# Three float32r score passes, half of a 31-tap convolution on GpSimd, and an earlier second GLU in a two-block layer kernel

## The chip, the cores and the metric

The kernel runs on one core of a Trainium2 chip. The metric is the device time of one execution in microseconds, the median of several runs. Everything is float32 at the interface; products are done in float32r, in pairs of a high and a low part, or in plain fp32.

## The reference, cut to what matters

Two transformer layers run over 512 tokens of width 1024. The change lies in the second layer's mixer. Its input projection gives a gated 3-tap convolution branch, a GLU branch with a 31-tap causal depthwise convolution over 256 channels, and eight heads of stick-breaking attention of width 64:

```
a_b, a_c, a_h, b_glu, q, k, v = split(rmsnorm(x) @ w_in)
y_a = a_b * causal_dwconv(a_c * a_h, w_conv_a)                  # 3 taps, 256 channels
g   = b_glu[:, :256] * sigmoid(b_glu[:, 256:])
g   = causal_dwconv(g, w_conv_b) + b_conv_b                     # 31 taps, 256 channels
y_b = silu(layernorm(g, ln_b_g, ln_b_b))
for each head and each block of 128 queries:
    z = q k^T / 8;  mask = key < query
    log_1m = where(mask, log_sigmoid(z) - z, 0)
    a = where(mask, exp(log_sigmoid(z) + sum of log_1m over later keys), 0)
    y_c = a @ v
x = x + concat(y_a, y_b, y_c) @ w_out;  x = x + relu(rmsnorm(x) @ w_ff1)^2 @ w_ff2
```

## The kernel before, in words

Weights come in tiles of 512 KB on SyncE's DMA queue (four staging buffers `wst`). Each tile is split into two float32r parts: ScalarE casts the high part `whi` (L113), VectorE subtracts to get the low part `wlo` (L114). A product with a weight tile is three float32r passes for each K tile of 128: high by high, high by low, low by high. Eight K tiles make one accumulation in a PSUM bank.

Engines run their own queues in order. The framework puts the instructions of the program in each engine's queue and adds the waits; a tile with a tag and a number of buffers makes a later writer wait for the last reader of the buffer.

The stick-breaking stage is written as interleaved generators. `sb_scores(h)` makes one head's weights, one step for each of four query tiles j of 128 x 128(j+1) scores. TensorE makes the scores `z` from `QF` and `KF` in plain fp32 (L937; it runs as two instructions) and adds the mask by a bf16 product with the identity (L938). ScalarE takes Abs, Exp and Ln of them (L942 to L944), VectorE makes log sigmoid in `sbL` (L946) and sums along the keys with a scan into `sbe` (L947), GpSimd zeroes the last column of `sbP` (L949), and ScalarE takes the last Exp (L950). `sb_values(h)` transposes the weights on TensorE, splits them into `PTh` and `PTl` (ScalarE and VectorE) and multiplies by the values `VB`; the last key tile goes through plain fp32 copies, `PTf` and `VB3`, L964. `pv_evac` adds the halves of the result `o` into `sby`.

Between these steps the generator `fill` puts independent work on TensorE, one K tile (three 512-column products) a step: the values of all heads (32 steps), then q and k of head pairs 1 to 3 (16 each), the second GLU (16), the two gated convolutions (24 each) and a part of the output projection (16): 160 in all. Thirty-two of them run beside head 0's scores, then 16 in each of the heads 0 to 7. The first pair's q and k and the first GLU are made before the stage.

The 31-tap convolution of one channel half `a` is a first tap (`tensor_scalar`, L1039) and 30 more (`scalar_tensor_tensor` of G, a tap's weight and `cb`, L1041), all on VectorE. `conv_taps` issues them one after another: three in each of the four steps before head 0, two in each of four steps of a head, half 1 behind half 0. At head 5 the rest is issued, and `ln_steps` transposes `cb` on TensorE (L1048) for the LayerNorm. `gate_steps` uses the buffers `gac` and `gam`.

```
fill = sequence(v_steps(), pair_steps(1), glu_steps(1), pair_steps(2), pair_steps(3), gate_steps(0),
                gate_steps(1), half_steps(yT, w_out_2, [4, 5, 0, 1], fin_add, 0))
for h in range(8):
    for j in range(4):
        steps(values); steps(fill, 2); conv_taps(1)
        steps(scores); steps(values); steps(fill, 2); conv_taps(1)
```

Of the kernel before, what the change touches and what calls it, by code (L numbers as in the profile page):

```python
# [20 lines left out]
def kernel(  # L21
# [42 lines left out]
    x = x[0]  # L64
# [35 lines left out]
    # the tensor engine's clock rises under load: products of zeros while the inputs are on their way  # L100
# [42 lines left out]
    def proj_T(acc, w, hT, cols=slice(0, 128), ts=slice(0, 512)):  # L143
        """acc[c, tok] = w[:, cols]^T h^T, the weights stationary."""
        wh, wl = w
        xh, xl = hT
        nk = wh.shape[1]
        for k in range(nk):
            mm(acc[:, ts], wh[:, k, cols], xh[:, k, ts], start=k == 0, stop=False)  # L149
            mm(acc[:, ts], wh[:, k, cols], xl[:, k, ts], start=False, stop=False)  # L150
            mm(acc[:, ts], wl[:, k, cols], xh[:, k, ts], start=False, stop=k == nk - 1)  # L151
# [5 lines left out]
    def k_steps(acc, w, hT):  # L157
        """the same, in steps of one K tile"""
# [6 lines left out]
    def first_tiles(tiles, ahead=()):  # L165
        """The first products after a norm: all of the first 256 tokens, while the others are still on their way."""
# [12 lines left out]
    def nat_mm(aT, acc, t, chunks, mid=lambda: None, cols=slice(None)):  # L179
        """acc[tok tile t, c] = sum_k a^T[k]^T w[k]; chunks: (list of k, split weights)"""  # L180
# [10 lines left out]
    def nat_steps(aT, acc, t, chunks):  # L191
        """nat_mm in steps of one K tile"""
# [17 lines left out]
    def natural(aT, w, ks, fin, c0=0, parts=None):  # L210
        """fin(t, half, acc) for both halves of 1024 columns, token tile by token tile."""
        for half in range(2):
            nat_half(aT, w, ks, fin, half, c0, parts)

    def nat_half(aT, w, ks, fin, half, c0=0, parts=None):
# [4 lines left out]
        for t in range(4):  # L220
            if t == 3 and half and parts:
                # in two, so that less is left to do after the last product
# [12 lines left out]
    def half_sq(src, half, st):  # L235
        """mean of squares of one half row; eps goes in with the first half"""
# [22 lines left out]
    def norm_T(t, g, hT):  # L259
        """RMS norm of token tile t of the residual, transposed into hT."""  # L260
# [18 lines left out]
    # transposes that wait for their norm: products that need not wait go first  # L279
# [9 lines left out]
    # =====================  block 1: mixers  =====================  # L289
# [86 lines left out]
    # transposed, with a row of ones for the bias  # L376
# [23 lines left out]
    def r_proj(hd):  # L400
        """x (1 + tanh(x / 2)) = 2 silu(x) of this head's output gate, natural layout"""
# [244 lines left out]
    def nsa_scores(h, bi):  # L646
        """softmax weights of one branch, gated; a step per query tile"""
# [27 lines left out]
    def nsa_values(h, bi):  # L675
        """the branch's weighted values, on top of the other branches'; a step per key tile and its products"""
# [46 lines left out]
    def merge_gates():  # L723
        """the gates of both mixers, in steps of one K tile"""
# [15 lines left out]
    # mn's tiles 2 p, 2 p + 1 take the place of the queries of heads 2 p, 2 p + 1  # L740
# [39 lines left out]
    for m in range(8):  # L780
# [3 lines left out]
        # the gated sum of both branches: one half of silu's and one of the gates' tanh form  # L784
# [7 lines left out]
    def post_norm_T(t, half, src, f, g, g_next, hT, st, eng):  # L792
        """x[t] += rms_norm(src) * g, then the next norm; src is one half of a token tile's row."""
# [22 lines left out]
    # =====================  block 1: FFN  =====================  # L816
    pc, tc3 = pool("pc")
    # 4 KB each: the first weights of block 2, then parts of its mixers' output
# [3 lines left out]
    # constants of block 2's mixers  # L822
# [66 lines left out]
    # =====================  block 2: mixers  =====================  # L889
    p3, t3 = pool("p3")  # L890
    # y^T as hi / lo: K tiles 0-1 the gated conv, 2-3 the GLU conv, 4-7 the attention
# [5 lines left out]
    QF, KF = {}, {}  # L897
    VB = [base.tile([128, 8, 2, 64], F32R, name="VB", tag="gain" if t < 2 else "xn", bufs=2) for t in range(4)]
    VB3 = t3("VB3", shape=(128, 8, 64))
# [4 lines left out]

    def pair_qk(i, accs):
        QF[i], KF[i] = t3("QF", bufs=2), t3("KF", bufs=2)
        A.activation(QF[i], accs[0], AF.Copy, scale=0.125)
        A.copy(KF[i], accs[1])

    def pair_steps(i):  # L910
        accs = []
        yield from tile_steps(accs, 1280 + i * 128)
        QF[i] = t3("QF", bufs=2)
        A.activation(QF[i], accs[0], AF.Copy, scale=0.125)
        yield from tile_steps(accs, 1792 + i * 128)
        KF[i] = t3("KF", bufs=2)
        A.copy(KF[i], accs[1])

    def v_steps():
        chunks = [([k, k + 1], load(w_in_2, k, 2, 2304, 512)) for k in range(0, 8, 2)]  # L920
        for t in range(4):
# [4 lines left out]
            if t == 3:  # L926
                A.copy(VB3, src)

    def sb_scores(h):
        """stick-breaking weights of one head, a step per query tile"""  # L930
# [3 lines left out]
        for j in range(4):  # L934
            n = 128 * (j + 1)
            z = ps("s", "z")
            mm(z[:, 0:n], QF[i][r, j * 128:(j + 1) * 128], KF[i][r, 0:n], start=True, stop=False)  # L937
# [7 lines left out]
            # log sigmoid(z); then -log a(s) = (z(s+1) - log a(s+1)) - log sigmoid(z(s)), from the masked end  # L945
# [3 lines left out]
            P.memset(p[:, n - 1:n], 0.0)  # L949
# [4 lines left out]
    def sb_values(h):  # L954
        """the head's output: a step per key tile and its products, those one tile behind"""
# [6 lines left out]
        def products(b, ph, pl):  # L962
            if b == 3:
                mm(o[0:64, 384:512], VB3[:, h, :], ph, start=False, stop=False)  # L964
                return
# [5 lines left out]
        for b in range(4):  # L971
# [4 lines left out]
            if b < 3:  # L976
                ph = t3("PTh", F32R, bufs=2)
                pl = t3("PTl0", F32R) if b == 0 else t3("PTl", F32R, bufs=2)
                split_psum(ph[:, 0:n], pl[:, 0:n], pt[:, 0:n])
                parts.append((b, ph, pl))  # L980
                pl0 = pl if b == 0 else pl0
            else:
                pf = t3("PTf", shape=(128, 128))
                A.copy(pf, pt[:, 0:n])
                parts.append((b, pf, None))
# [8 lines left out]
        pv_evac(o, sby[0][r], t3("pvt", shape=(64, 512)))  # L994
# [15 lines left out]
    def log_sigmoid(dst, src, e):  # L1010
        """min(x, 0) - ln(1 + exp(-|x|))"""
# [5 lines left out]
    def sigmoid(src):  # L1017
        th = t3("gth")
# [17 lines left out]
    def conv_b(a, k):  # L1036
        src = G[a][:, 2 + k:514 + k]
        if k == 0:
            V.tensor_scalar(cb[a], src, cwb[:, a, 0:1], cvec[:, 0, a:a + 1], op0=OP.mult, op1=OP.add)  # L1039
        else:  # L1040
            V.scalar_tensor_tensor(cb[a], src, cwb[:, a, k:k + 1], cb[a], OP.mult, OP.add)  # L1041

    def ln_steps():
        ln = []
        for t in range(4):
# [8 lines left out]
            # the convolution's inputs are used up  # L1054
# [15 lines left out]
    def gate_steps(a):  # L1070
# [5 lines left out]
        m = t3("gam", shape=(128, 544))  # L1076
# [13 lines left out]
    taps = [(a, k) for a in range(2) for k in range(31)]  # L1090

    def conv_taps(n):
        for _ in range(n):
            if taps and taps[0][0] in ready:
                conv_b(*taps.pop(0))
# [13 lines left out]
    fill = sequence(v_steps(), pair_steps(1), glu_steps(1), pair_steps(2), pair_steps(3), gate_steps(0),  # L1109
# [7 lines left out]
    for h in range(8):  # L1117
        scores = sb_scores(h + 1) if h < 7 else iter(())
        values = sb_values(h)
        for j in range(4):  # L1120
            steps(values)
            steps(fill, 2)
# [7 lines left out]
            steps(fill, 2)  # L1130
# [18 lines left out]
    # =====================  block 2: FFN  =====================  # L1149
# [87 lines left out]
```

## Time and profile before

| | |
|---|---|
| Median of three runs | 1508.88 us (1506.49, 1508.88, 1509.02) |
| Span of the profiled execution | 1504.9 us (its own time is not listed apart) |
| TensorE busy | 1487.9 us, 99% |
| VectorE busy | 765.6 us, 51% |
| ScalarE busy | 606.6 us, 40% |
| GpSimd busy | 62.9 us, 4% |
| The stick-breaking stage | about 937 to 1107 us |

The busy share is an average over stages with other limits: VectorE's 51% is far higher in the stage that the change touches. Matmuls are pipelined and their recorded ends are modelled, so the distance between starts tells more of TensorE than the durations. In the rows below the unit is the microsecond unless a mean is given in ns.

### The profile page before, as it was taken

The numbers are of one execution on the slowest core, as the hardware profiler recorded it, in microseconds if no ns is written. First come the engines' busy times: TensorE is split into PE (matmuls) and PEld (weight loads), VectorE is DVE, ScalarE is ACT, GpSimd is POOL, SyncE is SP. The second block draws the span as 40 slices with busy tenths as digits, with TensorE's granted clock in tenths as the row PEclk, the third lists the DMA queues.
The fourth block names the chain that finished last, engine by engine and source line by source line (L and its number), as shares of the span: only waits on it lengthen the run. The fifth ranks groups of instructions, "written<-read, shape, count | busy, mean of one in ns | idle before, by whom it ended". The sixth has DMA issues, their size and how long they took to land.

```text
span 1504.9 us, 18389 instructions
## 1 busy us (share of the span) xinstructions
PE 1487.9 (99%) x7220; PEld 1200.7 (80%) x7220; DVE 765.6 (51%) x1258; ACT 606.6 (40%) x1081; POOL 62.9 (4%) x177
## 2 busy tenths in 40 slices
PE   8999999999999999999999999999999999999998
PEld 6788888787788898878888888666689888888886
DVE  5244456867655463233333445979756344243343
ACT  6333224666632342322222334577734224142233
POOL 2000002000000010000000021000100000000000
PEclk9999999999999999999999999999999999999999
DMA  8242222221134243242243322211133242242321
GB/s 237 64 112 57 71 71 70 57 57 44 55 112 139 85 128 97 75 123 84 71 125 95 116 70 72 84 56 57 56 98 99 71 126 87 67 127 84 101 82 56
DMA packets 181278, 133.09 MB, mean 88 GB/s; under 512 B 11765, under 2 KB 157239, under 8 KB 181192
## 3 DMA queue, kind: packets, MB, share of 16 engines
q1 hardware_dynamic: 181192, 131.92, 30.2%
q8 instruction: 57, 0.93, 0.3%
q14 instruction: 29, 0.24, 0.1%
HBM read 129.80 MB, written 2.10 MB: 88 GB/s over the span
## 4 chain that ended last, share of the span: by engine, by line
PE 94%; DVE 2%; POOL 1%; ACT 1%; issue 1%; SPq 0%; DMA 0%; POOLq 0%; ACTq 0%; DVEq 0%
PE ps L149 13%; PE ps L151 13%; PE ps L150 13%; PE nat L187 9%; PE nat L186 9%; PE nat L185 9%; PE ps L162 4%; PE ps L161 4%; PE ps L160 4%; PE z L937 1%; PE pt L700 1%; PE ps L187 1%; PE ps L185 1%; PE ps L186 1%; PE o L693 1%; PE tp L273 1%
## 5 line engine op out<-in xcount | busy, mean ns | idle before, releaser
L113 ACT CAST whi<-wst 128x1024 fp32r<-128x1024 f32 (+1 forms) x229 | 239.1, 1046 | 493.6 <-PE ps L150 196.2
L114 DVE TENSOR_TENSOR wlo<-wst,whi 128x1024 fp32r<-128x1024 f32 (+1 forms) x229 | 279.5, 1222 | 287.1 <-ACT whi L113 283.4
L149 PE MATMUL ps<-hTh,whi 128*128 128x512 f32 (+1 forms) x880 | 331.4, 377 | 0.0
L150 PE MATMUL ps<-hTl,whi 128*128 128x512 f32 (+1 forms) x880 | 330.2, 375 | 0.0
L151 PE MATMUL ps<-hTh,wlo 128*128 128x512 f32 (+1 forms) x880 | 329.4, 374 | 0.0
L151 PEld LDWEIGHTS ps<-hTh,wlo 128*128 128x128 f32 x880 | 165.7, 188 | 31.9 <-DVE wlo L114 0.2
L149 PEld LDWEIGHTS ps<-hTh,whi 128*128 128x128 f32 x880 | 165.7, 188 | 31.6
L150 PEld LDWEIGHTS ps<-hTl,whi 128*128 128x128 f32 x880 | 165.8, 188 | 30.9
L187 PE MATMUL nat<-whi,al 128*128 128x512 f32 (+1 forms) x440 | 171.7, 390 | 0.0
L186 PE MATMUL nat<-wlo,ah 128*128 128x512 f32 (+1 forms) x440 | 171.4, 389 | 0.0
L185 PE MATMUL nat<-whi,ah 128*128 128x512 f32 (+1 forms) x440 | 170.9, 388 | 0.0
L160 PE MATMUL ps<-hTh,whi 128*128 128x512 f32 x240 | 98.0, 408 | 0.0
L186 PEld LDWEIGHTS nat<-wlo,ah 128*128 128x128 f32 x440 | 82.8, 188 | 18.6
L185 PEld LDWEIGHTS nat<-whi,ah 128*128 128x128 f32 x440 | 82.8, 188 | 18.3
L187 PEld LDWEIGHTS nat<-whi,al 128*128 128x128 f32 x440 | 82.8, 188 | 17.5
L161 PE MATMUL ps<-hTl,whi 128*128 128x512 f32 x240 | 96.2, 401 | 0.0
L162 PE MATMUL ps<-hTh,wlo 128*128 128x512 f32 x240 | 95.8, 399 | 0.0
L1087 DVE TENSOR_TENSOR xt<-xt,nat 128x512 f32<-128x512 f32 x43 | 29.5, 686 | 98.9 <-PE nat L187 97.6
L162 PEld LDWEIGHTS ps<-hTh,wlo 128*128 128x128 f32 x240 | 45.3, 189 | 8.8
L240 POOL TENSOR_SCALAR sq<-sq 128x1 f32<-128x1 f32 x28 | 9.4, 335 | 1015.9 <-ACT junk L238 1015.5
L865 DVE TENSOR_TENSOR sg<-sg,ps 128x512 f32<-128x512 f32 x22 | 15.2, 689 | 70.6 <-PE ps L151 69.9
L160 PEld LDWEIGHTS ps<-hTh,whi 128*128 128x128 f32 x240 | 45.4, 189 | 6.5
(351 smaller groups left out, 2194.8 us busy)
## 6 DMA issues: line engine op xcount, KB each, us to landing
wst<-in_w_in_dram SPq DMA_DIRECT2D x70, 512.0 KB, 3.9
wst<-in_w_ff_dram SPq DMA_DIRECT2D x64, 512.0 KB, 4.0
wst<-in_w_ffn_gate_dram SPq DMA_DIRECT2D x22, 512.0 KB, 4.0
wst<-in_w_ffn_up_dram SPq DMA_DIRECT2D x22, 512.0 KB, 4.0
wst<-in_w_ffn_down_dram SPq DMA_DIRECT2D x22, 512.0 KB, 3.8
wst<-in_w_out_dram SPq DMA_DIRECT2D x16, 512.0 KB, 3.9
xt<-in_x_dram SPq DMA_DIRECT2D x8, 512.0 KB, 3.6
wst<-in_w_proj_gla_dram SPq DMA_DIRECT2D x8, 512.0 KB, 3.6
```

The source lines that it names most:

```text
L113: A.copy(hi, st)
L114: lo_eng[0].tensor_tensor(out=lo, in0=st, in1=hi.bitcast(F32), op=OP.subtract)
L149: mm(acc[:, ts], wh[:, k, cols], xh[:, k, ts], start=k == 0, stop=False)
L150: mm(acc[:, ts], wh[:, k, cols], xl[:, k, ts], start=False, stop=False)
L151: mm(acc[:, ts], wl[:, k, cols], xh[:, k, ts], start=False, stop=k == nk - 1)
L160: mm(acc, w[0][:, k], hT[0][:, k], start=k == 0, stop=False)
L161: mm(acc, w[0][:, k], hT[1][:, k], start=False, stop=False)
L162: mm(acc, w[1][:, k], hT[0][:, k], start=False, stop=k == 7)
L185: mm(acc, ah[:, s], wh[:, j, cols], start=i == 0, stop=False)
L186: mm(acc, ah[:, s], wl[:, j, cols], start=False, stop=False)
L187: mm(acc, al[:, s], wh[:, j, cols], start=False, stop=i == len(seq) - 1)
L1087: V.tensor_tensor(X[t][:, HALF[half]], X[t][:, HALF[half]], acc, OP.add)
```

## The change

Queries and keys are split into high and low float32r parts (`QH`, `QL`, `KH`, `KL`), and a score tile is three float32r passes instead of one fp32 product. The last key tile of the values goes the same float32r way as the others; `VB3` and `PTf` go. The zeroed column of `sbP` is written by VectorE. Channel half 0 of the 31-tap convolution is done on GpSimd, each tap as a multiply into `tap` and an add into `cb`; half 1 stays on VectorE; `conv_taps` issues one tap of each half that is ready. The second GLU goes ahead of pair 1 in `fill`, and head 0 takes 32 steps of `fill`, the other heads 14 each. Some tiles share buffers (`pvt` with `PTl0`, `gam` with `gth`, `tap` with `gac`). The other lines of the diff only take comments out.

```
+    def split_q(i, acc):
+        QF[i] = t3("QH", F32R, bufs=2), t3("QL", F32R, bufs=2)
+        split_psum(*QF[i], acc, scale=0.125)
+    def split_k(i, acc):
+        KF[i] = t3("KH", F32R, bufs=2), t3("KL", F32R, bufs=2)
+        split_psum(*KF[i], acc)
...
-            if t == 3:
-                A.copy(VB3, src)
...
-            mm(z[:, 0:n], QF[i][r, j * 128:(j + 1) * 128], KF[i][r, 0:n], start=True, stop=False)
+            for a, b in ((0, 0), (0, 1), (1, 0)):
+                mm(z[:, 0:n], QF[i][a][r, j * 128:(j + 1) * 128], KF[i][b][r, 0:n], start=a + b == 0, stop=False)
...
-            P.memset(p[:, n - 1:n], 0.0)
+            V.memset(p[:, n - 1:n], 0.0)
...
-            if b == 3:
-                mm(o[0:64, 384:512], VB3[:, h, :], ph, start=False, stop=False)
-                return
...
-        pv_evac(o, sby[0][r], t3("pvt", shape=(64, 512)))
+        pv_evac(o, sby[0][r], t3("pvt", shape=(64, 512), tag="PTl0"))
...
+        eng = V if a else P
         if k == 0:
-            V.tensor_scalar(cb[a], src, cwb[:, a, 0:1], cvec[:, 0, a:a + 1], op0=OP.mult, op1=OP.add)
+            eng.tensor_scalar(cb[a], src, cwb[:, a, 0:1], cvec[:, 0, a:a + 1], op0=OP.mult, op1=OP.add)
+        elif a:
+            V.scalar_tensor_tensor(cb[a], src, cwb[:, a, k:k + 1], cb[a], OP.mult, OP.add)
         else:
-            V.scalar_tensor_tensor(cb[a], src, cwb[:, a, k:k + 1], cb[a], OP.mult, OP.add)
+            tap = t3("tap", tag="gac")
+            P.tensor_scalar(tap, src, cwb[:, a, k:k + 1], None, op0=OP.mult)
+            P.tensor_tensor(out=cb[a], in0=cb[a], in1=tap, op=OP.add)
...
-    fill = sequence(v_steps(), pair_steps(1), glu_steps(1), pair_steps(2), pair_steps(3), gate_steps(0),
+    fill = sequence(v_steps(), glu_steps(1), pair_steps(1), pair_steps(2), pair_steps(3), gate_steps(0),
...
-            steps(fill, 2)
+            steps(fill, 2 if h else 4)
...
-            steps(fill, 2)
+            steps(fill, 2 - j % 2 if h else 4)
```

TensorE's queue at the widest score tile of head 0 (`z` from keys and queries, `identb` and `smask` the mask, then the values' projection), the piece of the difference:

```order
-L937 MATMUL z<-KF,QF 128x512
-L938 LDWEIGHTS identb
-L938 MATMUL z<-smask,identb 128x128
+L940 MATMUL z<-KH,QH 128x512
+L940 MATMUL z<-KL,QH 128x512
+L940 MATMUL z<-KH,QL 128x512
+L941 LDWEIGHTS identb
+L941 MATMUL z<-smask,identb 128x128
```

The one fp32 product has become three passes at the same place; the mask stays behind them.

GpSimd's queue at the start of the stage (`sq` and `rstd` belong to the norm before it, `sbP` are weight tiles, `G_7399` is half 1's input), before:

```order
L949 MEMSET sbP_7987 128x1
L1031 MEMSET G_7399 128x32
L1077 MEMSET gam 128x32
L240 TENSOR_SCALAR sq<-sq 128x1
L245 TENSOR_TENSOR rstd<-sq 128x1
L246 TENSOR_TENSOR rstd<-rstd,nhalf 128x1
L949 MEMSET sbP_8041 128x1
```

and now (`G_7397` is half 0's input and `cb_7395` its sum, `G_7398` half 1's input):

```order
L1026 MEMSET G_7398 128x32
L240 TENSOR_SCALAR sq<-sq 128x1
L245 TENSOR_TENSOR rstd<-sq 128x1
L246 TENSOR_TENSOR rstd<-rstd,nhalf 128x1
L1035 TENSOR_SCALAR cb_7395<-G_7397,cwb,cvec 128x512
L1040 TENSOR_SCALAR tap<-G_7397,cwb 128x512
L1041 TENSOR_TENSOR cb_7395<-cb_7395,tap 128x512
L1040 TENSOR_SCALAR tap<-G_7397,cwb 128x512
L1041 TENSOR_TENSOR cb_7395<-cb_7395,tap 128x512
```

The one-column memsets have gone from this queue, and the pair of multiply and add follows the first tap thirty times in a row; the memset of `gam` stands behind them.

VectorE's queue in head 1, from the sum of head 0's values (`sby`) on, before:

```order
L644 TENSOR_TENSOR sby<-o,pvt 64x512
L947 SCALAR_TENSOR_TENSOR sbe<-z,sbL 128x511
L114 TENSOR_TENSOR wlo<-wst,whi 128x1024
L946 SCALAR_TENSOR_TENSOR sbL<-z,sbe 128x128
L947 SCALAR_TENSOR_TENSOR sbe<-z,sbL 128x127
L138 TENSOR_TENSOR PTl_8017<-pt,PTh 128x512
L138 TENSOR_TENSOR PTl<-pt,PTh 128x384
L946 SCALAR_TENSOR_TENSOR sbL<-z,sbe 128x256
L947 SCALAR_TENSOR_TENSOR sbe<-z,sbL 128x255
L114 TENSOR_TENSOR wlo<-wst,whi 128x1024
L138 TENSOR_TENSOR PTl<-pt,PTh 128x256
L1015 SCALAR_TENSOR_TENSOR gth<-ps,gth 128x512
```

and now, at the same place (`cb_7396` is half 1's sum):

```order
L644 TENSOR_TENSOR sby<-o,pvt 64x512
L138 TENSOR_TENSOR KL<-ps,KH 128x512
L138 TENSOR_TENSOR PTl_8152<-pt,PTh 128x512
L1037 SCALAR_TENSOR_TENSOR cb_7396<-G_7398,cwb,cb_7396 128x512
L952 MEMSET sbP_8372 128x1
L114 TENSOR_TENSOR wlo<-wst,whi 128x1024
L949 SCALAR_TENSOR_TENSOR sbL<-z,sbe 128x128
L138 TENSOR_TENSOR PTl<-pt,PTh 128x384
L950 SCALAR_TENSOR_TENSOR sbe<-z,sbL 128x127
L1037 SCALAR_TENSOR_TENSOR cb_7396<-G_7398,cwb,cb_7396 128x512
L952 MEMSET sbP_8426 128x1
```

In head 1 half 1's taps were not yet there, since its GLU (`gth`, L1015) lay in this head; now they stand between the scans and splits, with `KL` and the memsets.

## Rows read from the trace of the kernel before

**Rows 1.** The page, parts 1 and 2: busy time by engine; TensorE's granted clock.
```profile
PE 1487.9 (99%) x7220; PEld 1200.7 (80%) x7220; DVE 765.6 (51%) x1258; ACT 606.6 (40%) x1081; POOL 62.9 (4%) x177
...
PEclk9999999999999999999999999999999999999999
```
**Rows 2.** Stretches: length, busy PE, PEld, DVE, ACT, POOL, clock, DMA share, GB/s.
```profile
999.00:1017.00 18.00, 18.00 (x81) 12.04 (x80) 17.18 (x27) 11.85 (x26) 0.39 (x4) 1.00 0.20 58
...
1035.00:1053.00 18.00, 18.00 (x82) 12.24 (x81) 16.97 (x27) 12.93 (x26) 0.39 (x4) 1.00 0.21 61
```
**Rows 3.** Order of time, TensorE, widest score: start, duration, engine, line, tiles, shapes.
```profile
955.68 0.39 PE L199 MATMUL ps<-whi,hTl 128*128 128x512 f32 x1
956.00 1.12 PE L937 MATMUL z<-KF,QF 64*128 64x512 f32 x2
957.06 0.23 PE L938 MATMUL z<-smask,identb 128*128 128x128 bf16 x1
957.10 0.48 PE L197 MATMUL ps<-whi,hTh 128*128 128x512 f32 x1
957.42 0.39 PE L198 MATMUL ps<-wlo,hTh 128*128 128x512 f32 x1
...
962.29 0.39 PE L198 MATMUL ps<-wlo,hTh 128*128 128x512 f32 x1
```
**Rows 4.** The same view at a score tile of 128 columns.
```profile
964.68 0.40 PE L162 MATMUL ps<-hTh,wlo 128*128 128x512 f32 x1
965.01 0.49 PE L937 MATMUL z<-KF,QF 64*128 64x128 f32 x2
965.43 0.23 PE L938 MATMUL z<-smask,identb 128*128 128x128 bf16 x1
...
965.78 0.39 PE L161 MATMUL ps<-hTl,whi 128*128 128x512 f32 x1
```
**Rows 5.** The same view: float32r products of 256 columns.
```profile
936.07 0.28 PE L150 MATMUL ps<-hTl,whi 128*128 128x256 f32 x1
936.19 0.28 PE L151 MATMUL ps<-hTh,wlo 128*128 128x256 f32 x1
```
**Rows 6.** Order of time, TensorE's weight loads around a float32r product of 64 columns.
```profile
249.08 0.19 PEld L583 LDWEIGHTS ps<-hTh,whi 128*128 128x128 f32 x1
249.19 0.19 PEld L615 LDWEIGHTS sc<-KC,QSp 128*128 128x128 f32 x1
```
**Rows 7.** Order of time, TensorE, the last key tile's value product of head 0.
```profile
979.72 0.40 PE L162 MATMUL ps<-hTh,wlo 128*128 128x512 f32 x1
980.05 0.43 PE L964 MATMUL o<-PTf,VB 128*64 128x128 f32 x2
980.41 0.50 PE L991 MATMUL o<-PTl,VB 128*128 128x512 f32 x1
```
**Rows 8.** VectorE's groups, 937 to 1107 us: tiles, shapes, count | busy us, mean ns.
```profile
L1041 DVE SCALAR_TENSOR_TENSOR cb<-G,cwb,cb 128x512 f32<-128x512 f32 x60 | 44.7, 744 | 0.8
L114 DVE TENSOR_TENSOR wlo<-wst,whi 128x1024 fp32r<-128x1024 f32 x21 | 25.5, 1216 | 3.5 <-ACT whi L113 3.4
...
L138 DVE TENSOR_TENSOR VB<-ps,VB 128x512 fp32r<-128x512 f32 x4 | 2.8, 688 | 0.3 <-ACT VB L137 0.2
```
**Rows 9.** Order of time, GpSimd and VectorE, around 880 us.
```profile
880.22 1.30 POOL L795 TENSOR_TENSOR FA<-FA,gain 128x512 f32<-128x512 f32 x1
880.82 1.78 DVE L114 TENSOR_TENSOR wlo<-wst,whi 128x1024 fp32r<-128x1024 f32 x1 [1.81 <-ACT whi L113]
```
**Rows 10.** Order of time, GpSimd and VectorE, around 230 us.
```profile
229.25 0.74 POOL L562 TENSOR_SCALAR_AFFINE_SELECT negd<-negd 128x512 f32<-128x512 f32 x1
230.90 0.69 DVE L577 SCALAR_TENSOR_TENSOR QSp<-ps,QSp 64x512 fp32r<-64x512 f32 x1 [0.66 <-ACT QSp L576]
```
**Rows 11.** One line, L605: durations in ns (least/median/most), first and last start, shapes.
```profile
L605 POOL TENSOR_SCALAR biasc<-negc x8: 522/530/1197, 230.4 to 235.0; 128x128 f32<-128x128 f32 x8
```
**Rows 12.** The same view of L1048, the LayerNorm's transposes.
```profile
L1048 PE MATMUL lt<-ident,cb x8: 271/272/300, 1053.2 to 1062.2; 128*128 128x128 f32 x8
```

More of the change, by code (lines that the diff above doesn't have):

```diff
@@ L898 @@
     VB = [base.tile([128, 8, 2, 64], F32R, name="VB", tag="gain" if t < 2 else "xn", bufs=2) for t in range(4)]
-    VB3 = t3("VB3", shape=(128, 8, 64))
     def tile_steps(accs, c0):
@@ L903, in tile_steps @@
         yield from k_steps(accs[-1], load_cols(w_in_2, c0), hT)
+    def split_q(i, acc):
[4 more added lines that the diff above has]
+        split_psum(*KF[i], acc)
     def pair_qk(i, accs):
-        QF[i], KF[i] = t3("QF", bufs=2), t3("KF", bufs=2)
-        A.activation(QF[i], accs[0], AF.Copy, scale=0.125)
-        A.copy(KF[i], accs[1])
+        split_q(i, accs[0])
+        split_k(i, accs[1])
     def pair_steps(i):
@@ L912, in pair_steps @@
         yield from tile_steps(accs, 1280 + i * 128)
-        QF[i] = t3("QF", bufs=2)
-        A.activation(QF[i], accs[0], AF.Copy, scale=0.125)
+        split_q(i, accs[0])
         yield from tile_steps(accs, 1792 + i * 128)
-        KF[i] = t3("KF", bufs=2)
-        A.copy(KF[i], accs[1])
+        split_k(i, accs[1])
     def v_steps():
@@ L975, in sb_values @@
                 nc.tensor.transpose(pt[:, (j - b) * 128:(j - b + 1) * 128], pts[j][:, b * 128:(b + 1) * 128], ident)
[L976 to L985, printed above, removed]
+            ph = t3("PTh", F32R, bufs=2)
+            pl = t3("PTl0", F32R) if b == 0 else t3("PTl", F32R, bufs=2)
+            split_psum(ph[:, 0:n], pl[:, 0:n], pt[:, 0:n])
+            parts.append((b, ph, pl))
+            pl0 = pl if b == 0 else pl0
             yield
@@ L1017, in sigmoid @@
     def sigmoid(src):
-        th = t3("gth")
+        th = t3("gth", shape=(128, 544))[:, 0:512]
         log_sigmoid(th, src, th)
@@ L1075, in gate_steps @@
         c = t3("gac")
-        m = t3("gam", shape=(128, 544))
+        m = t3("gam", shape=(128, 544), tag="gth")
         P.memset(m[:, 0:32], 0.0)
@@ L1089 @@
     ready = set()
-    taps = [(a, k) for a in range(2) for k in range(31)]
+    taps = [[(a, k) for k in range(31)] for a in range(2)]
     def conv_taps(n):
         for _ in range(n):
-            if taps and taps[0][0] in ready:
-                conv_b(*taps.pop(0))
+            for a in ready:
+                if taps[a]:
+                    conv_b(*taps[a].pop(0))
     def yT(k):
```

## The prediction

> **What bounds the kernel now.** I read the page's busy shares first, then the busy time in stretches of the stick-breaking stage, then TensorE's instructions one by one, and last VectorE's and GpSimd's where they overlap. TensorE is busy 99% of the span at a granted clock of nine tenths or more, the 2.4 GHz level, all along [rows 1], so its in-order stream is the time: the change gains what it shortens in that stream and loses what it makes the stream wait. VectorE is the second engine here: in the three heads from 999 to 1053 us it is busy 17.1 of every 18 us while TensorE has no gap; ScalarE is busy 12 to 13 [rows 2]. GpSimd does almost nothing.
>
> **TensorE: what the score passes save.** A pass's price is its effect on the starts behind it, since recorded durations overlap. A k-step of three 512-column float32r products takes 0.696 us (seven between 957.42 and 962.29), so 0.232 each [rows 3]. The widest score pushes the second product behind it to 1.74 us after the product before it instead of 0.464, so it costs 1.28; the narrowest costs 1.10 - 0.464 = 0.64 [rows 3, 4]; the two between lie on that line, 0.85 and 1.06. One head: 3.83.
>
> After, three float32r passes and the mask product. The mask costs 0.04 to the next start and 0.09 more to the one after, 0.13 [rows 3]. A 256-column pass takes 0.12 [rows 5], a 512-column one 0.232, a 384-column one 0.175 between them. No float32r pass of 128 columns stands in the trace. Two bounds: 0.11, the spacing of two weight loads where a short product stands between long ones [rows 6], and 0.21, one of the two fp32 instructions at that width [rows 4]. I take 0.11, since it is a float32r row. Heads then cost 0.83 + 0.66 + 0.49 + 0.46 = 2.44 (2.74 by the other bound), saving 1.39 (1.09), or 11.1 (8.7) over eight heads.
>
> The last key tile's value product falls from 0.69 - 0.23 = 0.46 [rows 7] to two short passes, 0.22 (0.42): 1.9 (0.3) over eight heads. TensorE saves 13.0 us, 9.0 at the least.
>
> **VectorE: what it gets and in what time.** Per head and without taps it has 17.1 less ten taps at 0.744, so 9.7 [rows 2, 8]. The change adds QL or KL for 1.75 projection tiles (14 fill steps of 8) at 0.69, 1.2, priced by the same operation on VB; the last tile's PTl, a quarter of that width, 0.3; four one-column memsets, 0.2 as an estimate; and takes off a quarter of a 1.22 us wlo, 0.3 [rows 8]. That is 11.1 plus taps. Channel half 1 alone stays here, but the second GLU moved to the front makes it begin in the middle of head 0; the order has 12 taps in the rest of head 0, then 8, 7 and 4. Heads 1 to 3 need 17.1, 16.3 and 14.1 us.
>
> TensorE needs less than before: 18.0, less two fill steps moved into head 0 (1.4), less 13.0 / 8 = 1.6, so 15.0 a head. The rest of head 0 has 16 fill steps, 11.1, and half of a head's other work, (15.0 - 14 x 0.696) / 2 = 2.6: 13.7. VectorE there has half of 11.1, 12 taps (8.9), the product and first tap (1.2) and a wlo more (1.2), 16.8. So even unhindered VectorE is late by 3.1 + 2.1 + 1.3 = 6.5. Two PSUM banks of scores let it lag about one and a half score tiles, 15.0 / 4 x 1.5 = 5.6. The 31 taps taken off VectorE thus don't free the heads that matter: many ran before in the first 42 us of the stage.
>
> **GpSimd beside VectorE: the wait that the change adds.** Half 0 becomes 31 multiplies and 30 adds in one chain on GpSimd. An add of this shape takes 1.30 [rows 9]. The multiply has no row: 0.74 for one input at that shape [rows 10] is one end, 2.1 the other: four times the 0.53 of a tensor_scalar over 128 elements [rows 11]. I take 0.74, the same shape. Sum: 22.9 + 39.0 = 61.9 us.
>
> In rows 9 VectorE's wlo began while GpSimd's add ran and took 1.78 instead of the usual 1.22 [rows 8]: 0.56 lost. An operation with one input in PSUM didn't lose: 0.69 in the middle of GpSimd's series of 230.4 to 235 us [rows 10, 11], like VB's 0.69. So the taps and wlo, both inputs in SBUF, pay; scans, sbL, QL and PTl don't. GpSimd waits in turn. GpSimd starts near 940; by 973, when G of half 1 is there (48 fill steps and some 3 us), VectorE's eight wlo have held it 9.7, so 23 are done and 39 left. The rest of head 0 and head 1 give it 13 and 14 between VectorE's taps and wlo; it ends in the last third of head 2, about 1035. Until then 14 + 10 + 7 = 31 VectorE operations meet it: 31 x 0.56 = 17.4 us. Behind each stand the scans and splits that TensorE waits for. Ends: 0 if they never meet, and 31 x 1.02 (a whole mean GpSimd operation) = 31.6.
>
> The Trainium skill, "SBUF — State Buffer", Who interferes with whom, says that such an operation of VectorE and a GpSimd one that reads SBUF exclude each other, the loser waiting for the whole instruction. The trace's one pair agrees but for size: the add had 0.70 us left, by the rule 31 x 0.70 = 21.7 and 1519 us, by the row 17.4. The Trainium skill, "GPSIMD Engine Reference", Engine selection, calls one-input operations roughly line-rate; at the page's 1.2 GHz 512 elements are 0.43 us, an estimate by which GpSimd would need 52 and some 26 operations meet it, for 1511. The 0.53 us on 128 elements [rows 11] speak against that rule.
>
> **What is hidden.** The second GLU's loads, casts and products change place with pair 1's, one for one, on SP, ScalarE and TensorE. Head 0 draws four weight tiles, not two; the DMA share is 0.20 [rows 2]. ScalarE keeps its count, less VB3's copy, and its 12 to 13 us fit 15.0. `pvt` now shares PTl0's buffer, but the split that fills it stands behind the sum that reads it. The tap's buffer is also the gate's `gac`, wanted at the end of head 4, and the LayerNorm transposes, at 1053.2 now [rows 12], want the finished taps a little after; GpSimd is done by 1035. If not, these wait: rival C.
>
> **The sum.** VectorE is late 6.5 + 17.4 and may lag 5.6: TensorE stalls 18.3. Saved 13.0. Net +5.3 on the span of 1504.9, 1510.2. The runs' median, 1508.88, is 4.0 above the span; the execution profiled has no time of its own listed, and the runs lie 1.6 to 4.1 above. With 4.0: 1514 us.
>
> **Rivals.** A is the forecast. B: the engines rarely meet, because GpSimd's operations fall into the gaps that VectorE leaves; stall 6.5 - 5.6 = 0.9, net -12.1, 1497. For it: VectorE has a gap of some 5% in every head, and only one pair in the trace shows the loss. Against it: GpSimd's chain has no gap of its own, so a tap can't miss it often. B takes over from A where the loss per operation falls under (13.0 + 5.6 - 6.5) / 31 = 0.39. D: the loss lies just there, 0.30 to 0.48, and both sides cancel: 1509. C: the multiply takes 2.1, so GpSimd needs 104, plus 47 in which VectorE holds it (31 taps, twenty wlo), and ends near 1091. A's transposes would stand at 1053 + 8 fill steps (5.6) - 9 saved so far + 18 = 1067; TensorE waits 24 more there, 1538. For it: the 0.53 for 128 elements. Against it: those eight write strided slices, and the one-input row of the tap's own shape took 0.74. The change doing nothing is excluded for the passes: they are in TensorE's order, and rows of their kind are shorter.
>
> **How the numbers follow.** A 0.47, B 0.27, D 0.18, C 0.08. A's ends: no wait and 13.0 saved is B's 1497; a whole operation's wait, 31.6, with 9.0 saved is 6.5 + 31.6 - 5.6 - 9.0 = +23.5, 1532. The range 1498 to 1530 leaves out C and the tips. Around A alone it is 1511 to 1526. About 3 us (0.2%) is what a measurement can tell from no change. Faster is B and a little of D, 0.28; within 0.2% the rest of D and A's low edge, 0.19; slower 0.53.
>
> **What would show it.** Right: wlo and cb rows on VectorE with means well over 1.22 and 0.744 while GpSimd works, GpSimd's chain lasting some 95 us for 62 of work, gaps on TensorE before scores and transposes in heads 0 to 2, none from head 4 on, score passes gone from 30.6 to about 20 us. Wrong: VectorE's means unchanged (B), the multiply near 2 us and the gap at the LayerNorm transposes (C), or 128-column passes at 0.21 (4 us less saved).

## The result and the profile after

The changed kernel takes 1523.12 us (median of 4 runs, 1521.81 to 1524.3) beside 1508.15 for the kernel before on the same chip: ratio 1.0105, 95% interval 1.0091 to 1.0119. It is 15.0 us slower; 1514 was forecast, so the side was right and the size too small. The profiled execution of the changed kernel took 1522.78 us, its span is 1520.9.

The page of the changed kernel, busy time by engine (answers to [rows 1]):

```profile
PE 1491.2 (98%) x7252; PEld 1208.1 (79%) x7252; DVE 763.9 (50%) x1275; ACT 605.3 (40%) x1080; POOL 158.9 (10%) x206
```

GpSimd has 96 us more and VectorE hardly less: 31 taps went (some 23 us), some 10 us of splits and one-column memsets came, and what stayed got 12 us longer. Over the span this looks harmless. Stretches show it (columns as in [rows 2]); first the whole stage of the kernel before, then, for the changed one, the whole stage, two stretches of 15 us behind waits, and two of 2 us within them:

```profile
937.00:1133.00 196.00, 195.00 (x866) 138.77 (x866) 157.22 (x240) 119.38 (x239) 10.02 (x40) 1.00 0.24 70
```

```profile
937.00:1133.00 196.00, 182.59 (x826) 133.69 (x826) 147.78 (x238) 114.71 (x229) 103.84 (x72) 0.97 0.22 65
...
990.00:1005.00 15.00, 9.49 (x36) 6.38 (x34) 12.46 (x16) 4.77 (x9) 14.24 (x9) 0.77 0.24 72
1095.00:1110.00 15.00, 13.00 (x48) 8.46 (x47) 11.53 (x20) 9.78 (x23) 0.12 (x1) 0.77 0.12 35
...
999.00:1001.00 2.00, 2.00 (x5) 1.11 (x4) 2.00 (x5) 0.14 (x1) 1.82 (x3) 0.50 0.04 12
...
1099.00:1101.00 2.00, 2.00 (x6) 1.31 (x6) 1.95 (x6) 1.26 (x5) 0.00 (x0) 0.50 0.69 246
```

Length less busy time is idle time: 1.0 us before, 13.4 after, 12.4 more. The clock's loss is busy time times one less the granted clock, added up over stretches of 2 us: 0.0 before, 6.0 after. It stands in two places, each right behind a wait of TensorE, where the granted clock is 0.50, the lower level of 1.2 GHz. Together 18.4 us are listed as lost, and the span grew by 16.0: by this count the new products saved only 2.4. The count is a lower end, since not every lost step is listed as idle: in experiment 4, which has the products of before, the span grew by 7.0 with some 5.5 listed.

The largest wait, one timeline for TensorE, VectorE, ScalarE and GpSimd of the changed kernel, head 1 (start, duration, operation, in brackets the idle time before it and its releaser):

```profile
992.14 0.40 PE L160 MATMUL ps<-hTh,whi 128*128 128x512 f32 x1
998.05 0.48 PE L975 MATMUL pt<-ident,sbP 128*128 128x128 f32 x1 [5.51 <-ACT sbP L953]
...
989.24 0.73 DVE L1037 SCALAR_TENSOR_TENSOR cb<-G,cwb,cb 128x512 f32<-128x512 f32 x1
989.90 1.21 DVE L114 TENSOR_TENSOR wlo<-wst,whi 128x1024 fp32r<-128x1024 f32 x1
991.04 2.87 DVE L1037 SCALAR_TENSOR_TENSOR cb<-G,cwb,cb 128x512 f32<-128x512 f32 x2
993.84 0.68 DVE L949 SCALAR_TENSOR_TENSOR sbL<-z,sbe 128x512 f32<-128x512 f32 x1
994.44 1.70 DVE L1037 SCALAR_TENSOR_TENSOR cb<-G,cwb,cb 128x512 f32<-128x512 f32 x1
996.06 1.21 DVE L950 TENSOR_TENSOR_SCAN sbe<-z,sbL 128x511 f32<-128x511 f32 x1
...
997.36 0.63 ACT L953 ACTIVATE sbP<-sbe 128x511 f32<-128x511 f32 x1 [5.08 <-DVE sbe L950]
...
990.04 2.23 POOL L1041 TENSOR_TENSOR cb<-cb,tap 128x512 f32<-128x512 f32 x1
```

The page names ScalarE; the chain of waits goes one step further, to VectorE. Three taps that should take 0.74 each take 4.6 together and stand ahead of the scan for which ScalarE, and behind it TensorE, waits. They are the end of a longer row: from 980 us on, with VectorE busy 15.9 of 16 us, the ten taps ahead of this scan take 12.4 instead of 7.4. The 5.0 between is nearly the whole wait of 5.51; without GpSimd's taps 0.46 of it is left (experiments 1 and 6). VectorE's and GpSimd's groups in the stage (937 to 1125 us; answers to [rows 8]), and the scan of the kernel before (937 to 1107 us):

```profile
L1037 DVE SCALAR_TENSOR_TENSOR cb<-G,cwb,cb 128x512 f32<-128x512 f32 x30 | 31.8, 1060 | 0.3
L114 DVE TENSOR_TENSOR wlo<-wst,whi 128x1024 fp32r<-128x1024 f32 x21 | 27.9, 1336 | 3.7 <-ACT whi L113 3.6
L950 DVE TENSOR_TENSOR_SCAN sbe<-z,sbL 128x511 f32<-128x511 f32 x8 | 9.7, 1211 | 0.1
...
L1040 POOL TENSOR_SCALAR tap<-G,cwb 128x512 f32<-128x512 f32 x30 | 55.8, 1861 | 2.9
L1041 POOL TENSOR_TENSOR cb<-cb,tap 128x512 f32<-128x512 f32 x30 | 42.8, 1428 | 2.5
...
L947 DVE TENSOR_TENSOR_SCAN sbe<-z,sbL 128x511 f32<-128x511 f32 x8 | 9.7, 1211 | 0.0
```

The tap rose from 744 to 1060 ns and wlo from 1216 to 1336; the scan, with one input in PSUM, stayed at 1211. The Trainium skill ("SBUF — State Buffer", Who interferes with whom) says that an operation of VectorE with two SBUF inputs contends with a GpSimd one that reads SBUF, and one with at most one SBUF input doesn't. By which operations lose, the trace agrees.

The score passes are the other half of the miss. TensorE's products of one widest score of the changed kernel (answers to [rows 3]), and the weight loads of the same place:

```profile
956.02 0.40 PE L199 MATMUL ps<-whi,hTl 128*128 128x512 f32 x1
956.35 0.49 PE L940 MATMUL z<-KH,QH 64*128 64x512 f32 x1
956.68 0.39 PE L940 MATMUL z<-KL,QH 64*128 64x512 f32 x1
956.92 0.39 PE L940 MATMUL z<-KH,QL 64*128 64x512 f32 x1
957.25 0.23 PE L941 MATMUL z<-smask,identb 128*128 128x128 bf16 x1
957.28 0.48 PE L197 MATMUL ps<-whi,hTh 128*128 128x512 f32 x1
957.60 0.39 PE L198 MATMUL ps<-wlo,hTh 128*128 128x512 f32 x1
...
955.79 0.19 PEld L199 LDWEIGHTS ps<-whi,hTl 128*128 128x128 f32 x1
956.35 0.18 PEld L940 LDWEIGHTS z<-KH,QH 64*128 64x128 f32 x1 [0.37 <-issue]
956.46 0.19 PEld L940 LDWEIGHTS z<-KL,QH 64*128 64x128 f32 x1
```

A usual load begins one product ahead (955.79 for the product at 956.02). The first load of 64 rows begins with its own product, and steps of 0.33 instead of 0.23 stand before the first pass, before the second and before the mask.

The last key tile's value product in the changed kernel (compare [rows 7]):

```profile
990.42 0.40 PE L162 MATMUL ps<-hTh,wlo 128*128 128x512 f32 x1
...
990.83 0.45 PE L986 MATMUL o<-PTl,VB 128*128 128x512 f32 x1
```

From the product before to the one behind it is 0.41, where it was 0.69.

### The profile page after: what moved, and what is told of

Read it like the earlier page. It is cut to its first block, busy times and chain, and to the rows that moved or that the text cites. A ratio compares the mean times of both kernels' runs of the same rounds, so it can differ in the third digit from the quotient of the medians.

```text
span 1520.9 us, 18461 instructions
## 1 busy us (share of the span) xinstructions
PE 1491.2 (98%) x7252; PEld 1208.1 (79%) x7252; DVE 763.9 (50%) x1275; ACT 605.3 (40%) x1080; POOL 158.9 (10%) x206
## 4 chain that ended last, share of the span: by engine, by line
PE 89%; DVE 5%; ACT 2%; issue 2%; POOL 1%; SPq 0%; DMA 0%; POOLq 0%; ACTq 0%; DVEq 0%
PE ps L149 13%; PE ps L151 13%; PE ps L150 13%; PE nat L185 9%; PE nat L187 9%; PE nat L186 9%; PE ps L161 3%; PE ps L162 3%; PE ps L160 3%; PE pt L700 1%; PE ps L187 1%; PE ps L185 1%; PE ps L186 1%; PE o L693 1%; DVE cb L1037 1%
## 5 line engine op out<-in xcount | busy, mean ns | idle before, releaser
L187 PEld LDWEIGHTS nat<-whi,al 128*128 128x128 f32 x440 | 82.8, 188 | 18.4
L1040 POOL TENSOR_SCALAR tap<-G,cwb 128x512 f32<-128x512 f32 x30 | 55.8, 1861 | 2.9
```

The lines of the kernel that those rows point to most:

```text
L187: mm(acc, al[:, s], wh[:, j, cols], start=False, stop=i == len(seq) - 1)
L1040: P.tensor_scalar(tap, src, cwb[:, a, k:k + 1], None, op0=OP.mult)
```

## The experiments

Losses are over 937 to 1133 us as above. Each ratio is against the kernel before on the same chip.

**1. No taps on GpSimd.** The changed kernel without 30 of half 0's 31 taps (left out):

```diff
-            P.tensor_scalar(tap, src, cwb[:, a, k:k + 1], None, op0=OP.mult)
-            P.tensor_tensor(out=cb[a], in0=cb[a], in1=tap, op=OP.add)
+            pass
```

> The changed kernel without the 30 later taps of half 0 on GpSimd (its first tap stays; these taps are left out of the result). In the changed kernel VectorE's taps mean 1.06 us and its weight splits 1.34, TensorE stands idle 13.4 us in the stage, 7.5 of them before GpSimd ends, and runs some 11 us at half clock. Contention theory: taps go back to 0.74, splits to 1.22, the 5.5 us gap at the second head goes with its half-clock stretch, 1511 to 1514 us. Load theory (VectorE has too much to do there, whoever is beside it): the gap stays, 1520 to 1523. Thin-fill theory (14 steps of independent work a head are too few for the latency of a score's chain): the gaps of 0.5 to 1.4 us after 1045 us stay, so not under 1511.

Measured 1513.42, ratio 1.0041 (1.0026 to 1.0056). cb is 739 ns again, wlo 1217, and of the wait of 5.5 us 0.46 is left; idle 6.2, clock 3.4. So 9.7 of the 15.0 us hang on GpSimd's taps, as the contention theory has it; 5 to 6 do not. They stand at head 6, where waits of 1.34 and 0.63 and the clock's 3.4 stay: the thin-fill theory holds for them.

**2. The scores alone** (the kernel before with the float32r passes for scores and last key tile).

```diff
-            mm(z[:, 0:n], QF[i][r, j * 128:(j + 1) * 128], KF[i][r, 0:n], start=True, stop=False)
+            for a, b in ((0, 0), (0, 1), (1, 0)):
+                mm(z[:, 0:n], QF[i][a][r, ...], KF[i][b][r, 0:n], start=a + b == 0, stop=False)
```

> The kernel before with the float32r scores and the last key tile's float32r product alone. From the changed kernel's starts a score tile saves only 0.16 us at 512 columns, 0.10 at 384 and about as much below, since three passes on 64 rows have a step of 0.09 before them, between the first two and before the mask: 3 to 4 us in all. VectorE gets 1.5 us a head more and is at 17.1 of 18 already. Size theory: 1505 to 1509. If the passes were worth the 13 us of the prediction: 1496 to 1499. If VectorE's added splits make it late: 1510 to 1515.

1508.54, ratio 1.0008 (0.9999 to 1.0018). The size theory holds. The span grew by 1.6 us with 4.3 us more idle time and no clock loss: 2.7 saved by this count.

**3. GpSimd alone** (the kernel before with half 0 on GpSimd, and the one-column memset on VectorE).

```diff
+        eng = V if a else P
...
+            P.tensor_scalar(tap, src, cwb[:, a, k:k + 1], None, op0=OP.mult)
+            P.tensor_tensor(out=cb[a], in0=cb[a], in1=tap, op=OP.add)
```

> The kernel before with half 0 of the convolution on GpSimd alone (with the memset on VectorE), scores and fill order as before. VectorE's half 1 then starts in head 1, and fills lie 16 to a head. Contention theory: taps and weight splits are lengthened by 10 to 15 us in all; since VectorE has 31 taps less, TensorE waits less than in the changed kernel: 1509 to 1516, with VectorE's taps well over 0.74. If relief weighs more than waiting: 1505 to 1509. GpSimd's chain takes 88 us of its own and 15 to 20 of waiting, so it ends near 1045, before the LayerNorm transposes.

1520.79, ratio 1.009 (1.0075 to 1.0105), more than any theory had: cb 1008 ns, wlo 1416.

**4. The order alone** (the kernel before with the second GLU ahead of pair 1, 32 fill steps in head 0 and 14 in the others).

```diff
-            steps(fill, 2)
+            steps(fill, 2 if h else 4)
...
-            steps(fill, 2)
+            steps(fill, 2 - j % 2 if h else 4)
```

> The kernel before with only the order changed: second GLU ahead of pair 1, 32 fill steps in head 0 and 14 in the others. Thin-fill theory: TensorE gets gaps of about 1 us a head from head 1 on and perhaps a half-clock stretch, 1512 to 1518. Contention theory: nothing on GpSimd, so 1508 to 1511.

1513.93, ratio 1.0046 (1.003 to 1.0063): idle 3.2, clock 3.3, the latter and 2.1 of the idle time in one place at head 6: the thin-fill theory holds. The changed kernel has the same place; TensorE, VectorE and ScalarE there:

```profile
1094.93 0.39 PE L162 MATMUL ps<-hTh,wlo 128*128 128x512 f32 x1
1096.67 0.35 PE L940 MATMUL z<-KH,QH 64*128 64x256 f32 x1 [1.35 <-DVE sbe L950]
...
1094.10 0.69 DVE L949 SCALAR_TENSOR_TENSOR sbL<-z,sbe 128x512 f32<-128x512 f32 x1 [0.51 <-ACT sbe L947]
1095.31 1.21 DVE L950 TENSOR_TENSOR_SCAN sbe<-z,sbL 128x511 f32<-128x511 f32 x1
...
1093.44 0.63 ACT L947 ACTIVATE sbe<-sbe 128x512 f32<-128x512 f32 x1
```

GpSimd has long ended. The next score has no bank until the scan has read the last one, and the fill ahead of it is used up: between this score and the one before stand five fill steps, where the kernel before has seven. Two steps of 0.70 are 1.4, the wait 1.35.

**5. The fill as before** (the changed kernel with experiment 4's lines and the second GLU put back).

> The changed kernel with the fill in its old order and rate (pair 1 ahead of the second GLU, 4 steps per key tile); scores and GpSimd half as in the changed kernel. Alone, the parts cost about +13.0 us (GpSimd half), +6.8 (order and fill), +0.7 (scores), which is 20 where all three together cost 15: so two of them share their idle time. Theory that VectorE's lateness under contention is the one cause and that the thin fill only uncovers the same waits: about the time of the GpSimd half alone, 1519 to 1523, so that undoing the order gives back under 4 us. Rival, that the thin fill costs its own 6 to 7 us after GpSimd has ended: 1516 to 1517. Rival, that the three new passes per score are what makes TensorE wait with GpSimd at work: above 1523.

1517.96, ratio 1.0063 (1.0048 to 1.0078): 5.2 us come back, midway between the first two theories. At head 6 six fill steps stand in that place, and the wait there is gone. The cost of order and fill is mostly its own; what the earlier GLU costs without the thinner fill was not tested.

**6. Both halves on VectorE**, order and scores as changed.

```diff
-        eng = V if a else P
+        eng = V
...
+            if taps and taps[0][0] in ready:
+                conv_b(*taps.pop(0))
```

> The changed kernel with both halves of the convolution on VectorE, one behind the other as in the kernel before; scores, order and fill as in the changed kernel. VectorE gets 30 taps of 0.74 us (22 us) more than without GpSimd's taps at all (1513.4 us). Contention theory: the taps are 0.74 us again, they lie beside TensorE's work, and the time is that of the order alone or of the kernel without GpSimd's taps, 1513 to 1516. Rival, that VectorE's load is what makes the stage late and GpSimd relieved it of 22 us: at least as slow as the changed kernel, 1523 to 1535.

1514.79, ratio 1.0043 (1.0029 to 1.0057). The line of the taps in this kernel:

```profile
L1037 DVE SCALAR_TENSOR_TENSOR cb<-G,cwb,cb 128x512 f32<-128x512 f32 x60 | 44.5, 745 | 2.0 <-DVE cb L1037 1.2
```

VectorE with 60 taps is 8.3 us better than with 30 beside GpSimd; load is not the cause. The parts, against the kernel before: scores +1.5, GpSimd +13.7, order +6.8, scores and order +6.4, scores and GpSimd +9.6, all +15.0. They don't add. One difference among them bears on the passes: beside GpSimd's taps and in the old order the new products take the time from +13.7 to +9.6, 4.1 us less.

**7. Products of zeros in the wait.**

```diff
+            if h == 1 and b == 0:
+                for _ in range(22):
+                    mm(pt, identb, zerob, start=True, stop=True)
```

> The changed kernel with 22 products of zeros (128x512, bf16) that write the bank of head 1's first transposes just before them, where TensorE stood for 5.5 us and ran at half clock for some 6 us behind it; what the reference computes is unchanged. Theory that a stretch of idle costs twice, once as idle and once as the lower clock behind it: the clock's loss near 1000 us (2.6 us by the windows) goes, and the time falls by 1.5 to 3 us, to about 1520 to 1521.5. Rival, that TensorE would have waited for VectorE at the next transposes anyway: the clock stays high, idle grows by as much, and the time is the same, 1522.5 to 1523.7. Rival, that the products hold TensorE up at the half clock themselves: 1524 to 1527.

1527.96, ratio 1.0134 (1.0118 to 1.0149), 4.8 above the changed kernel, and all three theories fell: two by the time, the third because 21 of the products took 4.92, 0.23 each, the spacing of the higher clock. TensorE's waits in this kernel (this execution took 1531.06):

```profile
992.28 4.92 PE L978 MATMUL pt<-zerob,identb 128*128 128x512 bf16 x21
999.20 0.33 PE L980 MATMUL pt<-ident,sbP 128*128 128x128 f32 x1 [1.67 <-ACT sbP L955]
...
1010.30 0.44 PE L942 MATMUL z<-KH,QH 64*128 64x384 f32 x1 [1.54 <-DVE sbP L954]
...
1026.77 0.48 PE L980 MATMUL pt<-ident,sbP 128*128 128x128 f32 x1 [3.38 <-ACT sbP L955]
```

The lower clock near 1000 went, and came at 1011 and 1025 behind new waits; idle 13.7, clock 7.7, and the 4.9 of the zeros now count as busy. That the lower clock costs little where TensorE would wait for VectorE anyway fits the new waits, but isn't shown; why it became worse and not equal stays open.

**8. Two passes of 128 rows** (the kernel before; high and low part of a query stacked, against each key part twice).

```diff
-            mm(z[:, 0:n], QF[i][r, j * 128:(j + 1) * 128], KF[i][r, 0:n], start=True, stop=False)
+            for b in range(2):
+                mm(z[:, 0:n], QF[i, u][:, ...], KF[i, u][b][:, 0:n], start=b == 0, stop=False)
```

> The kernel before (both halves on VectorE, last key tile in fp32) with scores as two float32r passes of 128 rows: high and low part of the queries stacked on the partitions, against the keys' high part twice and low part twice, as the first block's NSA scores have it. The pair of heads 6 and 7 is projected after two thirds of the first gate's columns, so that its split finds the old tiles free; the gate's products leave their banks earlier. TensorE's work on scores falls from about 3.8 us per head to 1.5 to 1.9, 15 to 18 us over the eight heads; ScalarE gets about 14 us more (copies of 64 rows), VectorE about 11 (subtractions of 64 rows). Theory that TensorE's time sets the end as long as VectorE keeps up: 1494 to 1501. Rival, that with TensorE shorter VectorE (about 146 us busy in a stage of 170 before) and ScalarE set the pace, and the saving turns into idle TensorE and half clock as in the changed kernel: 1503 to 1512.

1510.79, ratio 1.0019 (1.0009 to 1.0028): the rival holds, idle 13.7, clock 2.7. Between 1076 and 1087 stand two long waits, 3.65 us behind ScalarE (the LayerNorm's `lny`) and 4.58 behind VectorE's scan.

**9. The same, spread out** (taps two per head earlier, LayerNorm one tile per key tile, SiLU in head 6).

```diff
-            conv_taps(1)
+            conv_taps(1 + j % 2)
...
-                steps(norm_b, 2)
+                steps(norm_b)
+            if h == 6 and j % 2 == 0:
+                steps(norm_b)
```

> The two wide passes per score again, with the convolution's end spread: the ten last taps go two per head earlier instead of in one piece at head 5, the LayerNorm's four transposes come one per key tile of head 5, and the two SiLU halves in head 6. In the two wide passes without this, TensorE stood 13.7 us in the stage and lost 2.7 us by the lower clock, of which 7.8 us stand in one stretch at 1077 to 1087 behind ScalarE (lny, sbe), and some 2.5 us at the LayerNorm before it. Theory that these waits are the pile of ScalarE and VectorE work at heads 5 and 6: they go, with the lower clock behind them, and the time falls by 7 to 11 us, to 1500 to 1504, faster than the kernel before. Rival, that ScalarE and VectorE are behind in the whole stage and TensorE waits for them elsewhere as soon as this pile is gone: 1507 to 1512.

1506.54, ratio 0.9999 (0.9990 to 1.0008), nearer to the rival: the long waits went, small ones came; idle 10.4, clock 1.5. The passes of 128 rows do what the three of 64 rows did not. A widest score here, and three stretches:

```profile
957.22 0.40 PE L199 MATMUL ps<-whi,hTl 128*128 128x512 f32 x1
957.45 0.39 PE L952 MATMUL z<-KSh,QS 128*128 128x512 f32 x1
957.68 0.40 PE L952 MATMUL z<-KSl,QS 128*128 128x512 f32 x1
957.92 0.23 PE L953 MATMUL z<-smask,identb 128*128 128x128 bf16 x1
957.96 0.48 PE L197 MATMUL ps<-whi,hTh 128*128 128x512 f32 x1
958.28 0.39 PE L198 MATMUL ps<-wlo,hTh 128*128 128x512 f32 x1
```

```profile
997.00:1017.00 20.00, 19.42 (x95) 15.14 (x96) 19.13 (x31) 16.07 (x33) 0.50 (x6) 1.00 0.14 40
1017.00:1037.00 20.00, 19.15 (x95) 14.17 (x94) 19.11 (x31) 17.15 (x38) 0.40 (x4) 1.00 0.14 41
1037.00:1057.00 20.00, 16.02 (x74) 11.26 (x73) 19.72 (x33) 13.45 (x28) 0.40 (x4) 1.00 0.17 51
```

No step is over 0.24 up to the mask; from product to product the score costs 1.06 - 0.464 = 0.60 instead of 1.28. VectorE is busy 58 of these 60 us; that it sets the pace is not shown, since of the 4.3 us of longer waits there 3.1 end with ScalarE.

**10. SiLU later** (experiment 9's last lines in the changed kernel).

> The changed kernel with the LayerNorm's transposes one per key tile of head 5 and its two SiLU halves in head 6, nothing else. Of its waits, those behind GpSimd's end (about 5.9 us of idle time and 3.3 us of lower clock) fall where the LayerNorm, the SiLU halves and the next heads' scores crowd ScalarE and VectorE. Theory that this crowd is what the thin fill uncovers: the late waits go for the most part, and the time falls by 5 to 8 us, to 1515 to 1518. Rival, that the fill is too thin by itself there, wherever the SiLU stands: 1521 to 1525.

1523.43, ratio 1.0103 (1.0087 to 1.0118): the rival holds. The late waits move from 1095 to 1099 to 1106; idle 14.2, clock 5.8.

**11. The multiply with two constants.**

```diff
-            P.tensor_scalar(tap, src, cwb[:, a, k:k + 1], None, op0=OP.mult)
+            P.tensor_scalar(tap, src, cwb[:, a, k:k + 1], zcol, op0=OP.mult, op1=OP.add)
```

> The changed kernel with GpSimd's multiply written with a second operation, mult by the tap's weight and add of a zero column, as its first tap is written (mult by the weight, add of the bias). In the changed kernel that first tap, with two constants, took 0.768 us with VectorE idle, and the multiply with one constant, same shape, same buffers' kind, 1.56 to 1.57 us in its first eight, most of which VectorE was idle beside: twice the 0.74 that the prediction had taken. Theory that the form of the operation with one constant costs the second 0.79 us: the multiply falls to 0.77 to 0.80 undisturbed, GpSimd's own work from 88 to about 64 us, its chain ends near 1020 instead of 1044.8, fewer of VectorE's operations meet it, and the time falls by 2 to 6 us, to 1517 to 1521. Rival, that the first tap is a special case (the first of a run) and the multiply stays at 1.57: 1522 to 1524.5. Rival, that the multiply is shorter but VectorE is held as long, since the faster engine meets it more often: multiply 0.77, chain shorter, time 1522 to 1524.5.

1523.72, ratio 1.0105 (1.0088 to 1.0122). First tap and a multiply alone, in the changed kernel, then here:

```profile
940.16 0.77 POOL L1035 TENSOR_SCALAR cb<-G,cwb,cvec 128x512 f32<-128x512 f32 x1 [19.36 <-DVE G L1028]
940.91 1.59 POOL L1040 TENSOR_SCALAR tap<-G,cwb 128x512 f32<-128x512 f32 x1
```

```profile
942.03 0.77 POOL L1042 TENSOR_SCALAR tap<-G,cwb,zcol 128x512 f32<-128x512 f32 x1
...
L1042 POOL TENSOR_SCALAR tap<-G,cwb,zcol 128x512 f32<-128x512 f32 x30 | 34.6, 1154 | 3.0
```

The form halves the multiply, and the chain ends at 1024.9 instead of 1044.9. The time stays: the third theory holds. The first twelve taps of VectorE, up to 1002 us, with those ahead of the largest wait among them, take 13.9 us in both kernels: what costs there is that they meet GpSimd, not how long GpSimd works after.

**12. Wide passes with GpSimd** (experiment 9 with half 0 on GpSimd as in 11, half 1 on VectorE from head 2 on, LayerNorm in head 6).

> The two wide passes per score with half 0 of the convolution on GpSimd in the two-constant form, in the order of the fill of the kernel before: half 1 becomes ready only at the end of head 1 (about 1005 us), GpSimd begins near 941 and by its undisturbed 0.77 + 1.30 us per tap plus some ten wlo that hold it is done near 1010 to 1020, so that VectorE's 31 taps hardly meet it; they go at 8 per head in heads 2 to 5, the LayerNorm to head 6, the SiLU halves to head 7; the one-column memsets and the GLU's memset are VectorE's. With the two wide passes spread out VectorE was busy 58 of 60 us from 997 to 1057 and TensorE, short of work by 13 us, waited 10.4 us and lost 1.5 by the lower clock. Theory that VectorE's load is what limits the wide passes and that the contention costs little where VectorE's own taps don't run beside GpSimd: VectorE loses 22 us of taps and gets some 3 to 5 back by contention, TensorE's waits fall under 5 us, and the time falls to 1497 to 1502, faster than the kernel before. Rival, that any GpSimd chain beside this stage costs 8 to 10 us whatever meets it, as in the changed kernel: 1506 to 1514. Rival, that the waits come from ScalarE and the score chain's own latency now that TensorE's head is short: 1503 to 1508.

1508.75, ratio 1.0006 (0.9997 to 1.0015). VectorE's taps hardly meet GpSimd (802 ns), yet wlo does (1438), and VectorE is busy 59.3 of the 60 us from 997 to 1057; idle 13.9. The theory fell; the time lies in the first rival's range and 0.75 above the second's, and which of the two holds stays open. No version beats the kernel before.

## Why the prediction was right, and where its sum failed

- **Mechanism: right. Side: right, in part by luck.** GpSimd beside VectorE makes taps and wlo longer, TensorE waits behind them (experiments 1, 3, 6). B is out: cb 1060 and wlo 1336 against 744 and 1216. C is out: the multiply is slower than taken, but the LayerNorm transposes come at 1068.0, 23 us after GpSimd's end. Yet with the 12.0 that VectorE lost (below) in place of 17.4, the sum itself gives 6.5 + 12.0 - 5.6 - 13.0 = -0.1, D's standstill. That the kernel is slower was brought about by two other terms that failed, the saving and the lateness without GpSimd.
- **The saved 13.0 us: the term that failed.** Some 4 came: 4.3 by the starts (2.1 by the scores, 2.2 by the last key tile, forecast 1.9), 4.1 by experiments 3 and 5, 2.4 to 2.7 by the listed losses, which leave steps out. For the widest score 0.83 was forecast and 957.60 - 956.02 - 0.464 = 1.12 measured; by the same spacing the others come to 0.96, 0.78 and 0.71 (forecast 0.66, 0.49, 0.46). A head falls from 3.83 to 3.57, 2.1 us over eight, not 11.1. The 128-column bound was not at fault: the second and third such pass follow each other in 0.11, as taken. I priced a pass at its spacing in a run of 128-row products; the steps into and out of 64 rows were in no row of float32r, but the first of them stands before the fp32 product of 64 rows, 0.32 and 0.33 in [rows 3, 4], and I left it out. Experiment 9 shows that at 128 rows they aren't there; why 64 rows cost them stays open.
- **The stall of 18.3 us: right in sum by luck, wrong in its parts.** 18.4 are listed as lost, but 6.0 of them by the lower clock, which the sum did not have. Contention was put at 17.4; taking it away gives 8.3 to 9.7 (experiments 6 and 1). 31 operations were to lose 0.56 each; the 30 taps and 21 wlo lost 30 x 0.316 + 21 x 0.120 = 12.0 us. Only 24 of them are longer than usual, by some 0.5 each: the price was nearly right, the number of meetings too high.
- **The lateness without GpSimd: too small and misplaced.** 6.5 less a lag of 5.6 was forecast for heads 0 to 2. Order and fill cost 5.2 to 6.8 (experiments 5 and 4), at head 6, where five fill steps instead of seven are used up before the scan is through; "none from head 4 on" is wrong.
- **GpSimd's multiply: 0.74 taken, 1.56 measured** undisturbed, and the chain 105 us where 95 was forecast. Experiment 11 shows that this changes nothing in the time.

So: net +5.3 forecast with 13.0 saved and 18.3 lost; +16.0 came with some 4 saved and some 20 lost, 18.4 of them listed. Most of the miss, about 9 of 10.7, is the saving.

## What to carry to other kernels

A product's price taken from a steady run of one shape doesn't hold where the number of rows changes at each use: look for a row of the mixed sequence, or stack to 128 rows. Work moved to GpSimd was not free here beside VectorE's operations with two SBUF inputs, and was beside its scans with one input in PSUM; ask which operation of the second busiest engine stands ahead of what the bound engine waits for. Thinner fill cost time where a score's chain was latest, far from where the steps were taken.

## What the runs showed of the hardware

- A GpSimd multiply of 128x512 by one per-partition constant took 1.56 us; with a second operation, an add of a per-partition constant, 0.77. The Trainium skill ("GPSIMD Engine Reference", Elementwise — side-by-side cycle accounting) gives 769 ns as the best case for 512 elements: the second form agrees, the first takes twice that.
- float32r products of 64 rows between products of 128 rows: three steps of about 0.10 us per score, with the first weight load not ahead of its product.
- The granted clock fell to 0.50 for about 6 us behind waits of 1.35 and 0.63 close together, as behind one of 5.5. It did so behind the same pair of waits in experiments 1, 6 and 7. In experiment 11 the same pair, 1.34 and 0.63, came at 1097 to 1101, and the clock stayed up:

```profile
1097.00:1112.00 15.00, 13.01 (x59) 8.53 (x59) 14.25 (x25) 10.41 (x24) 0.12 (x1) 1.00 0.11 38
```
